# Activation transposes of the feed-forwards: from TensorE to VectorE and a round trip through device memory

## The chip, the cores and the metric
The kernel runs on one core of a Trainium2 chip: TensorE (PE) with its weight loads (PEld), VectorE (DVE), ScalarE (ACT), GpSimd (POOL), SyncE (SP) and 16 DMA engines. The metric is the device time of one execution in microseconds. Before the change it is 1530.09 us, the median of 3 runs (1528.64 to 1535.28).

## The reference
A first block (RWKV-7 time mixing and differential attention side by side, a feed-forward, and PLE, a gated addition) is followed by two layers of a second block, each a gated feed-forward, an attention stage and another gated feed-forward. There are 256 tokens of width 1024, all in fp32. What the change touches is the five feed-forwards and PLE:

```
# first block; h = rmsnorm(x, norm_mlp_g)
x = x + square(relu(h @ w_ff1)) @ w_ff2                              # 1024 -> 4096 -> 1024
x = x + (p @ w_ple) * sigmoid(rmsnorm(x, norm_ple_g) @ w_ple_gate)
# second block, four times; h = rms_norm(x, g)
x = x + 0.5 * ((silu(h @ w_gate) * (h @ w_up)) @ w_down)             # 1024 -> 2816 -> 1024
```

## The kernel before
The tokens are two tiles of 128 (t = 0, 1, the token halves). A matmul wants its contraction on the partitions, so each left factor is needed transposed: `hT`, the normed input, and `aT`, the activations of a feed-forward. Every fp32 product is made of three matmuls (`mm3`): both factors are split into a high part `hi`, rounded to the type of the fast matmul, and the rest `lo`, and hi\*hi, hi\*lo and lo\*hi are added up in PSUM.

Weights come from device memory in units of 128x1024 (512 KB). SP's queue issues their transfers into three `raw` buffers; ACT makes `hi` (L365) and DVE `lo` (L366). There are 5 + 6 = 11 pairs of hi/lo buffers; a pair comes free when PE has read its unit for the last time. An up or gate block of 512 columns is four units of two rows of blocks; a down block of 512 rows is four units.

`mlp` goes through the hidden width in chunks of 512 (one of a gated feed-forward's six is 256 wide; the first feed-forward has eight). For each chunk it makes the up product of both token halves (gate and up products in a gated one), ACT evacuates the first product with its nonlinearity (L463) and DVE multiplies (L465); the result is `a`, 128 tokens by 512. `flip_side` makes `aT` of it: four PE transposes of 128x128 into a PSUM bank (L283), then ACT's `aTh` and DVE's `aTl` out of PSUM (L365, L366). The down product of a chunk (`down`) runs one chunk late, after the up products of the next chunk, into four PSUM banks that stay held. In chunk 0 the products are ordered by token half (t outer), in the others by weight (j outer).

PE's order is written out by the program: `Weave` keeps a modelled time, and side streams such as `flip_side` are put between the matmuls of the main stream once their due time has come (3.0 us after `a` was issued). The order on the other engines is made by a scheduler, and each engine takes its instructions in order. `Normed` makes `hT`: half of x is multiplied by the gain (L909, in `FinalNorm` L1751), flipped by PE, and its reciprocal norm `r` is applied when a product is evacuated. `Ple.run` makes the gate product of token half 0 with all of `w_ple_gate` (eight units), the value products of both halves, and the gate product of half 1; `merge` adds to x.

POOL has no transfer in this kernel; its few operations are in the mixing and attention stages.

Of the kernel before, what the change touches and what calls it, by code (L numbers as in the profile page):

```python
# [7 lines left out]
F32 = mybir.dt.float32  # L8
# [4 lines left out]
AF = mybir.ActivationFunctionType  # L13
ALU = mybir.AluOpType
# [4 lines left out]
D = 1024  # L19
# [89 lines left out]
class Mark:  # L109


    def __init__(self):
        self.done, self.at, self.res = False, 0.0, None
# [105 lines left out]
class Ker:  # L219


    def __init__(self, ctx, tc, d):
        self.tc, self.nc, self.d = tc, tc.nc, d
        nc = self.nc
        ctx.enter_context(tc.manual_schedule(engines={mybir.EngineType.PE}))
        self.W = Weave()
        self.const = ctx.enter_context(tc.tile_pool(name="const", bufs=1))
        self.xp = ctx.enter_context(tc.tile_pool(name="xp", bufs=1))
        self.act = ctx.enter_context(tc.tile_pool(name="act", bufs=2))
        self.ps = ctx.enter_context(tc.tile_pool(name="ps", bufs=1, space=PSUM))  # L230
        self.banks = Slots(self.W, self.ps, "b", [128, 512], 8)
        self.quota, self.held = 2, 0
        self.x = [self.xp.tile([128, D], F32, name=f"x{t}") for t in range(2)]
        self.pre = None
# [195 lines left out]
    def flip_side(self, src, hi, lo, lat, wait=()):  # L430
# [8 lines left out]
        s.res = (hi, lo)  # L439
        return s  # L440

    def mlp(self, pool, hT, names, i, chunks, kind, res, after):

        nc, W = self.nc, self.W
        self.quota = 6
        acc = {}
        held = []
        nw = len(names) - 1  # L450
        for ci, w in enumerate(chunks):
            kt = w // 128
            ws = [self.wblock((n, i, ci)) for n in names[:-1]]
            order = [(t, j) for t in range(2) for j in range(nw)] if ci == 0 else [(t, j) for j in range(nw) for t in range(2)]
            a, aT = {}, {}
            for t, j in order:
                b = self.bank()
                p = b[1][:, :w]
                for k in range(8):
                    self.mm3(p, hT[t].at(k), ws[j][k], k == 0, k == 7)  # L460
                if j == 0:
                    a[t] = pool.tile([128, 512], F32, tag="a", name="a", bufs=4)[:, :w]
                    nc.scalar.activation(out=a[t], in_=p, func=AF.Silu if kind == "swiglu" else AF.Relu, scale=hT[t].r)  # L463
                if j == nw - 1:
                    nc.vector.scalar_tensor_tensor(out=a[t], in0=p, scalar=hT[t].r, in1=a[t], op0=ALU.mult, op1=ALU.mult)  # L465
                    th = pool.tile([128, 4, 128], F32R, tag="aTh", name="aTh", bufs=5)
                    tl = pool.tile([128, 4, 128], F32R, tag="aTl", name="aTl", bufs=5)
                    aT[t] = self.flip_side(a[t], th[:, :kt], tl[:, :kt], 3.0)
                self.drop(b, 2.0)
            held.append((kt, aT, self.wblock((names[-1], i, ci))))  # L470
            if 1 <= ci < len(chunks) - 1:
                for t in range(2):
                    self.down(acc, t, held[:1], res)
                held = held[1:]
        for t in range(2):
            self.down(acc, t, held, res, after)
# [420 lines left out]
class Normed:  # L897
# [9 lines left out]
    def half(self, s, lat=3.0):  # L907
        c = slice(s * 512, s * 512 + 512)
        self.K.nc.vector.tensor_tensor(out=self.h[:, c], in0=self.K.x[self.t][:, c], in1=self.g[:, c], op=ALU.mult)  # L909
        self.flip(s, lat)  # L910
        self.K.square(self.K.x[self.t], s, self.ss)
        if s:
            self.m, self.r = self.K.rstd(self.ss, "x")
# [29 lines left out]
def ffn_plan(names, i, chunks):  # L943

    out, off = [], 0
    for ci, w in enumerate(chunks):
        for n in names[:-1]:
            out.append(((n, i, ci), (0, D), [(off, off + w)]))
        out.append(((names[-1], i, ci), (off, off + w), [(0, D)]))
        off += w  # L950
    return out
# [89 lines left out]

def first_plan():
    out = ffn_plan(("w_ff1", "w_ff2"), 0, FF1_CHUNKS)
    out.append((("w_ple_gate", 0, 0), (0, D), [(0, D)]))
    out.append((("w_ple", 0, 0), (0, 256), [(0, D)]))
    return out


# [4 lines left out]
class Mix:  # L1053
# [193 lines left out]
    def inverse(self, H, wait):  # L1247
# [25 lines left out]
        gl = lambda q, i: G[quad[q], 4 * H + i % 4, c_of(q, i), 32 * (q % 2):32 * (q % 2) + 32]  # L1273
        at = lambda T: (lambda q, i: T[quad[q], i])
        product(reg[0], at(U), at(L))
        nc.vector.tensor_tensor(out=X, in0=reg[0], in1=X, op=ALU.add)
        yield 0.8
        product(reg[1], at(U), at(X))
        nc.vector.tensor_tensor(out=X, in0=reg[1], in1=bc(self.i32), op=ALU.add)
        nc.vector.transpose(out=Y, in_=X)  # L1280
        yield 0.9
        for lv in range(3):
            product(reg[0], gl, at(X))
            nc.scalar.activation(out=Q, in_=reg[0], func=AF.Copy)
            yield 0.8
            product(reg[1], at(Y), at(Q))
            nc.vector.copy_predicated(out=X, mask=bc(self.lvl[:, lv]), data=reg[1])
            nc.vector.transpose(out=Y, in_=X)
            yield 1.3
# [400 lines left out]
class Ple:  # L1690
# [8 lines left out]
            lo = pool.tile([128, 2, 128], F32R, name="pTl", tag="pTl", bufs=2)  # L1699
            self.flips.append(K.flip_side(pt, hi, lo, 4.0))  # L1700

    def product(self, lhs, w, evacuate):
        K = self.K
        for s in range(2):
            c = slice(s * 512, s * 512 + 512)
            b = K.bank()
            n = len(w)
            for k in range(n):
                K.mm3(b[1], lhs(k), (w[k][0][:, c], w[k][1][:, c]), k == 0, k == n - 1)
            evacuate(s, c, b[1])  # L1710
            K.drop(b)

    def run(self, pool, hT, after):
        K, nc = self.K, self.K.nc
        K.quota = 4
        wg = K.wblock(("w_ple_gate", 0, 0))
        wp = K.wblock(("w_ple", 0, 0))
        gt = [pool.tile([128, D], F32, name="pg", tag="pg", bufs=2) for _ in range(2)]
        pw = pool.tile([128, D], F32, name="pw", tag="pw", bufs=1)

        def gate(t):
            self.product(hT[t].at, wg, lambda s, c, p: nc.scalar.activation(out=gt[t][:, c], in_=p, func=AF.Sigmoid, scale=hT[t].r))

        def value(t, evacuate):
            f = K.W.need(self.flips[t])
            self.product(lambda k: (f[0][:, k], f[1][:, k]), wp, evacuate)

        def merge(t, s, c, v):
            nc.vector.tensor_tensor(out=gt[t][:, c], in0=gt[t][:, c], in1=v, op=ALU.mult)
            nc.vector.tensor_tensor(out=K.x[t][:, c], in0=K.x[t][:, c], in1=gt[t][:, c], op=ALU.add)  # L1730
            after(t, s)

        gate(0)
        value(0, lambda s, c, p: merge(0, s, c, p))
        value(1, lambda s, c, p: nc.scalar.activation(out=pw[:, c], in_=p, func=AF.Copy))
        self.product(hT[1].at, wg, lambda s, c, p: (
            nc.scalar.activation(out=gt[1][:, c], in_=p, func=AF.Sigmoid, scale=hT[1].r), merge(1, s, c, pw[:, c])))


class FinalNorm(Normed):  # L1740
# [63 lines left out]
def full_plan():  # L1804
    return mix_plan() + first_plan() + second_plan()
# [48 lines left out]
```

## Time and profile before

| | |
|---|---|
| median of 3 runs | 1530.09 us |
| profiled execution | 1529.78 us, of which the span from the first to the last instruction is 1528.0 |
| granted TensorE clock, mean | 0.994 |
| busy: PE, PEld, DVE, ACT, POOL | 1489.4, 1237.2, 927.9, 760.8, 46.7 us |
| transfers | 253.53 MB on SP's queue, 51.1% of the 16 DMA engines' time |

The stages follow each other: mixing to about 300 us, the first feed-forward to 470, PLE to 501, then layer 0 (feed-forward to 685, attention to 817, feed-forward to 1015) and layer 1 (to 1199, to 1332, to the end). Matmuls are pipelined: the profile gives one of 512 columns some 0.39 us, and they start 0.23 us apart. An engine's idle time is given with what ended it (the releaser).

### The profile page before, as it was taken

The page shows a single profiled execution, that of the slowest core. Times are in us where ns is not written, and L with a number is a line of the kernel's source. Part 1 is how long each engine was busy: PE and PEld are TensorE (multiplying, and loading weights), DVE is VectorE, ACT ScalarE, POOL GpSimd, SP SyncE. Part 2 cuts the span into 40 slices and gives each one's busy share as a digit, 9 for nine tenths or more (in the row PEclk, how much of TensorE's full clock was granted, in tenths as well). Part 3 has the DMA queues.
Part 4 walks back from the last instruction along what each step waited for, and adds up shares of the span by engine and source line. Part 5 has one row for each costly group of instructions (what it writes and reads, how often), then busy time and mean ns, then how long its engine had stood idle before and what let it go on. Part 6 is the DMA issues. An engine that isn't in the chain of part 4 may idle for free.

```text
span 1528.0 us, 22440 instructions
## 1 busy us (share of the span) xinstructions
PE 1489.4 (97%) x8804; PEld 1237.2 (81%) x8804; DVE 927.9 (61%) x1528; ACT 760.8 (50%) x1142; POOL 46.7 (3%) x70
## 2 busy tenths in 40 slices
PE   7999989999999999999999999999999999999999
PEld 6887767788888788887888888887888888888887
DVE  5886777755558755557546554566545787565552
ACT  6644445644536544447565444445444566464441
POOL 1120100000000000001100000000000010000000
PEclk9999999999999999999999999999999999999999
DMA  7233238655544765536434665547555444275551
GB/s 253 90 118 107 98 119 278 202 194 177 182 151 157 223 200 190 185 132 193 138 111 147 198 194 192 179 156 220 190 189 182 141 154 136 78 227 180 179 182 53
DMA packets 76298, 254.97 MB, mean 167 GB/s; under 512 B 11040, under 2 KB 13344, under 8 KB 76192
## 3 DMA queue, kind: packets, MB, share of 16 engines
q1 hardware_dynamic: 76192, 253.53, 51.1%
q8 instruction: 69, 1.13, 0.3%
q14 instruction: 37, 0.30, 0.1%
HBM read 252.45 MB, written 1.05 MB: 166 GB/s over the span
## 4 chain that ended last, share of the span: by engine, by line
PE 81%; DVE 7%; DMA 5%; ACT 4%; issue 2%; POOL 0%; SPq 0%; ACTq 0%; DVEq 0%; POOLq 0%
PE b L279 77%; DMA raw<-in_w_dram 4%; PE b L283 4%; DVE lo L366 2%; ACT hi L365 2%; DMA grow<-in_norm_mix_g_dram 0%; DMA stage<-in_consts_dram 0%; DMA lam<-in_lam_k_dram 0%; POOL rb L563 0%; POOL rb L562 0%; DVE hTl L366 0%; DVE c L1132 0%; DVE U L1260 0%; DVE u L1129 0%; ACT e L376 0%
## 5 line engine op out<-in xcount | busy, mean ns | idle before, releaser
L366 DVE TENSOR_TENSOR lo<-raw,hi 128x1024 fp32r<-128x1024 f32 (+1 forms) x465 | 561.9, 1214 | 356.1 <-ACT hi L365 350.1
L365 ACT ACTIVATE hi<-raw 128x1024 fp32r<-128x1024 f32 (+1 forms) x465 | 485.6, 1050 | 417.4 <-PE b L279 207.6
L279 PE MATMUL b<-hi,hTh 128*128 128x512 f32 (+2 forms) x1312 | 499.9, 381 | 0.7 <-ACT hi L365 0.7
L279 PE MATMUL b<-hi,hTl 128*128 128x512 f32 (+2 forms) x1312 | 489.9, 373 | 0.5 <-DVE hTl L366 0.5
L279 PE MATMUL b<-lo,hTh 128*128 128x512 f32 (+2 forms) x1312 | 489.7, 373 | 0.8 <-DVE lo L366 0.8
L279 PEld LDWEIGHTS b<-hi,hTl 128*128 128x128 f32 x1312 | 247.4, 189 | 47.8 <-DVE hTl L366 0.9
L279 PEld LDWEIGHTS b<-hi,hTh 128*128 128x128 f32 x1312 | 247.6, 189 | 46.1 <-issue 2.5
L279 PEld LDWEIGHTS b<-lo,hTh 128*128 128x128 f32 x1312 | 247.8, 189 | 44.2 <-DVE lo L366 1.5
L279 PE MATMUL b<-hi,aTh 128*128 128x512 f32 x480 | 191.6, 399 | 0.0
L279 PE MATMUL b<-hi,aTl 128*128 128x512 f32 x480 | 188.1, 392 | 0.0
L279 PE MATMUL b<-lo,aTh 128*128 128x512 f32 x480 | 187.4, 390 | 0.0
L279 PEld LDWEIGHTS b<-hi,aTl 128*128 128x128 f32 x480 | 90.1, 188 | 20.1
L279 PEld LDWEIGHTS b<-lo,aTh 128*128 128x128 f32 x480 | 90.3, 188 | 18.0
L279 PEld LDWEIGHTS b<-hi,aTh 128*128 128x128 f32 x480 | 90.2, 188 | 17.6
L463 ACT ACTIVATE a<-b,rsi_x 128x512 f32<-128x512 f32 (+1 forms) x52 | 34.4, 662 | 55.3 <-PE b L279 55.2
L365 ACT ACTIVATE aTh<-b 128x512 fp32r<-128x512 f32 (+1 forms) x64 | 36.3, 567 | 43.2 <-PE b L283 41.8
L465 DVE SCALAR_TENSOR_TENSOR a<-b,rsi_x,a 128x512 f32<-128x512 f32 (+1 forms) x52 | 37.2, 716 | 32.1 <-PE b L279 17.3
L366 DVE TENSOR_TENSOR aTl<-b,aTh 128x512 fp32r<-128x512 f32 (+1 forms) x64 | 41.8, 653 | 20.0 <-ACT aTh L365 19.7
L279 PE MATMUL b<-hi,hT1h 128*128 128x512 f32 (+1 forms) x128 | 53.4, 418 | 0.0
L279 PE MATMUL b<-lo,hT1h 128*128 128x512 f32 (+1 forms) x128 | 47.8, 373 | 0.6 <-DVE lo L366 0.6
L279 PE MATMUL b<-hi,hT1l 128*128 128x512 f32 (+1 forms) x128 | 47.4, 371 | 0.0
L365 ACT ACTIVATE hTh<-b 128x512 fp32r<-128x512 f32 (+1 forms) x48 | 25.2, 541 | 38.1 <-PE b L283 33.5
(582 smaller groups left out, 1293.6 us busy)
## 6 DMA issues: line engine op xcount, KB each, us to landing
raw<-in_w_dram SPq DMA_DIRECT2D x446, 512.0 KB, 4.2
raw<-in_w_dram SPq DMA_DIRECT2D x16, 384.0 KB, 3.4
grow<-in_norm_ffn_dram SPq DMA_DIRECT2D x4, 512.0 KB, 5.3
x<-in_x_dram SPq DMA_DIRECT2D x4, 256.0 KB, 6.2
x<-in_x_dram SPq DMA_DIRECT2D x2, 512.0 KB, 4.4
grow<-in_norm_mix_dram SPq DMA_DIRECT2D x2, 512.0 KB, 4.8
out_dram<-x SPq DMA_DIRECT2D x4, 256.0 KB, 2.0
raw<-in_w_dram SPq DMA_DIRECT2D x2, 396.0 KB, 3.6
```

The lines of the kernel that those rows point to most:

```text
L279: self.nc.tensor.matmul(out=out, lhsT=lhsT, rhs=rhs, start=start, stop=stop, skip_group_check=skip)
L283: self.nc.tensor.transpose(out=out, in_=src, identity=self.ident)
L365: self.nc.scalar.activation(out=hi, in_=src, func=AF.Copy)
L366: self.nc.vector.tensor_tensor(out=lo, in0=src, in1=hi.bitcast(F32), op=ALU.subtract)
L463: nc.scalar.activation(out=a[t], in_=p, func=AF.Silu if kind == "swiglu" else AF.Relu, scale=hT[t].r)
L465: nc.vector.scalar_tensor_tensor(out=a[t], in0=p, scalar=hT[t].r, in1=a[t], op0=ALU.mult, op1=ALU.mult)
```

## The change
It has three parts. `flip_moved` takes the place of `flip_side` in every chunk of a feed-forward but the last: DVE transposes the 32x32 squares within each quarter of the partitions (L449), POOL's queue stores the tile to a buffer in device memory (L451, 512 pieces of 512 bytes) and reads it back in four transfers, one for each quarter of the partitions (L453, 128 pieces of 512 bytes each; half as long in the 256 wide chunk), and ACT and DVE make `aTh` (L455) and `aTl` (L456) from SBUF. PE's modelled time takes the result as ready 9.0 us later. Then, chunk 0 is ordered by weight like the others. Last, PLE's gate weight is cut into two blocks of 512 columns, its products are ordered by half block, and all four value products go through ACT to SBUF.

```
...
+        self.dram = ctx.enter_context(tc.tile_pool(name="dram", bufs=3, space=bass.MemoryType.DRAM))
...
+    def flip_moved(self, pool, src, hi, lo):
+
+        nc = self.nc
+        n = src.shape[1] // 128
+        sq = pool.tile([128, 4, 4, 32], F32, name="fsq", tag="fsq", bufs=2)[:, :, :n]
+        to = pool.tile([128, 4, 4, 32], F32, name="fto", tag="fto", bufs=2)[:, :, :n]
+        nc.vector.transpose(out=sq.rearrange("p j k s -> p k j s"), in_=src.rearrange("p (k j s) -> p k j s", j=4, s=32))
+        mid = self.dram.tile([4, 32, 4, 128 * n // 4], F32, name="fmid", tag=f"fmid{n}")
+        nc.gpsimd.dma_start(out=mid.rearrange("i r j e -> (i r) j e"), in_=sq.rearrange("p j k s -> p j (k s)"))
+        for j in range(4):
+            nc.gpsimd.dma_start(out=to[32 * j:32 * j + 32].rearrange("r i k s -> r i (k s)"), in_=mid[:, :, j].rearrange("i r e -> r i e"))
+        v = lambda x: x.rearrange("p k (i s) -> p i k s", s=32)
+        nc.scalar.activation(out=v(hi), in_=to, func=AF.Copy)
+        nc.vector.tensor_tensor(out=v(lo), in0=to, in1=v(hi).bitcast(F32), op=ALU.subtract)
+        m = Mark()
+        m.res = (hi, lo)
+        self.W.finish(m, 9.0)
+        return m
+
 
 
     def mlp(self, pool, hT, names, i, chunks, kind, res, after):
@@ -451,7 +471,7 @@
         for ci, w in enumerate(chunks):
             kt = w // 128
             ws = [self.wblock((n, i, ci)) for n in names[:-1]]
-            order = [(t, j) for t in range(2) for j in range(nw)] if ci == 0 else [(t, j) for j in range(nw) for t in range(2)]
+            order = [(t, j) for j in range(nw) for t in range(2)]
             a, aT = {}, {}
             for t, j in order:
                 b = self.bank()
@@ -465,7 +485,10 @@
                     nc.vector.scalar_tensor_tensor(out=a[t], in0=p, scalar=hT[t].r, in1=a[t], op0=ALU.mult, op1=ALU.mult)
                     th = pool.tile([128, 4, 128], F32R, tag="aTh", name="aTh", bufs=5)
                     tl = pool.tile([128, 4, 128], F32R, tag="aTl", name="aTl", bufs=5)
-                    aT[t] = self.flip_side(a[t], th[:, :kt], tl[:, :kt], 3.0)
+                    if ci == len(chunks) - 1:
+                        aT[t] = self.flip_side(a[t], th[:, :kt], tl[:, :kt], 3.0)
+                    else:
+                        aT[t] = self.flip_moved(pool, a[t], th[:, :kt], tl[:, :kt])
                 self.drop(b, 2.0)
             held.append((kt, aT, self.wblock((names[-1], i, ci))))
             if 1 <= ci < len(chunks) - 1:
...
 def first_plan():
     out = ffn_plan(("w_ff1", "w_ff2"), 0, FF1_CHUNKS)
-    out.append((("w_ple_gate", 0, 0), (0, D), [(0, D)]))
+    out.append((("w_ple_gate", 0, 0), (0, D), [(0, 512)]))
     out.append((("w_ple", 0, 0), (0, 256), [(0, D)]))
+    out.append((("w_ple_gate", 0, 1), (0, D), [(512, D)]))
     return out
 
 
...
-    def product(self, lhs, w, evacuate):
...
+    def product(self, lhs, w):
+        K = self.K
+        b = K.bank()
+        for k in range(len(w)):
+            K.mm3(b[1], lhs(k), w[k], k == 0, k == len(w) - 1)
+        return b
...
+        def value(t, s, wp):
             f = K.W.need(self.flips[t])
...
+            nc.scalar.activation(out=pw[t][:, c], in_=b[1], func=AF.Copy)
...
-        gate(0)
-        value(0, lambda s, c, p: merge(0, s, c, p))
-        value(1, lambda s, c, p: nc.scalar.activation(out=pw[:, c], in_=p, func=AF.Copy))
-        self.product(hT[1].at, wg, lambda s, c, p: (
-            nc.scalar.activation(out=gt[1][:, c], in_=p, func=AF.Sigmoid, scale=hT[1].r), merge(1, s, c, pw[:, c])))
+        w = K.wblock(("w_ple_gate", 0, 0))
+        wp = K.wblock(("w_ple", 0, 0))
+        gate(0, 0, w)
+        for s in range(2):
+            value(0, s, wp)
+        merge(0, 0)
+        gate(1, 0, w)
+        w = K.wblock(("w_ple_gate", 0, 1))
+        gate(0, 1, w)
+        merge(0, 1)
+        for s in range(2):
+            value(1, s, wp)
+        merge(1, 0)
+        gate(1, 1, w)
+        merge(1, 1)
...
```

Lines 1 to 231 keep their numbers; below them the changed kernel's are one higher, and from `mlp` on about twenty (L463 becomes L483, L465 becomes L485, L365 and L366 become L366 and L367).

On ACT, in a middle chunk of the first feed-forward (`a` is the evacuation of a product, `hi` the split of a weight unit, `aTh` the high part of the transposed activations, out of the PSUM bank `b` or the tile `fto` that was read back). Before:

```order
L463 ACTIVATE a<-b,rsi_x 128x512
L365 ACTIVATE hi<-raw 128x1024 x2
L365 ACTIVATE aTh<-b 128x512
L365 ACTIVATE hi<-raw 128x1024
L463 ACTIVATE a<-b,rsi_x 128x512
L365 ACTIVATE hi<-raw 128x1024
L365 ACTIVATE aTh<-b 128x512
L365 ACTIVATE hi<-raw 128x1024 x4
```

And now, in the same place:

```order
L483 ACTIVATE a<-b,rsi_x 128x512
L366 ACTIVATE hi<-raw 128x1024 x3
L483 ACTIVATE a<-b,rsi_x 128x512
L366 ACTIVATE hi<-raw 128x1024
L455 ACTIVATE aTh<-fto 128x4x4x32
L366 ACTIVATE hi<-raw 128x1024 x3
L455 ACTIVATE aTh<-fto 128x4x4x32
L366 ACTIVATE hi<-raw 128x1024
```

Both `aTh` now stand behind the second evacuation, the first with one split between and the second three splits later.

On ACT, in a full chunk of a gated feed-forward, before:

```order
L463 ACTIVATE a<-b,rsi_g 128x512
L365 ACTIVATE hi<-raw 128x1024 x3
L463 ACTIVATE a<-b,rsi_g 128x512
L365 ACTIVATE hi<-raw 128x1024 x3
L365 ACTIVATE aTh<-b 128x512
L365 ACTIVATE hi<-raw 128x1024 x2
L365 ACTIVATE aTh<-b 128x512
```

And now:

```order
L483 ACTIVATE a<-b,rsi_g 128x512
L366 ACTIVATE hi<-raw 128x1024 x3
L483 ACTIVATE a<-b,rsi_g 128x512
L366 ACTIVATE hi<-raw 128x1024 x5
L455 ACTIVATE aTh<-fto 128x4x4x32
L366 ACTIVATE hi<-raw 128x1024 x2
L455 ACTIVATE aTh<-fto 128x4x4x32
```

Two more splits stand ahead of the first `aTh`; the rest of the chunk is as before.

On POOL, at the end of layer 0's first feed-forward and the attention stage behind it (`rb` is part of the attention's rotary step). Before, this is all that POOL does there:

```order
L1391 TENSOR_TENSOR z<-z,row_g_1195 128x256
L562 TENSOR_TENSOR rb<-qn,gs 128x8x32
L563 TENSOR_TENSOR rb<-qn,gs 128x8x32
L562 TENSOR_TENSOR rb<-qn,gs 128x8x32
L563 TENSOR_TENSOR rb<-qn,gs 128x8x32
```

And now (`fmid` is the buffer in device memory, `fsq` the tile that DVE transposed):

```order
L451 DMA fmid<-fsq 128x512
L453 DMA fto<-fmid 32x4x128 x4
L451 DMA fmid<-fsq 128x512
L453 DMA fto<-fmid 32x4x128 x4
L585 TENSOR_TENSOR rb<-qn,gs 128x8x32
L586 TENSOR_TENSOR rb<-qn,gs 128x8x32
```

Each flip puts five transfers on POOL's queue, one store and four reads, of which the first read waits until the store has landed; nothing else of POOL stands among them in a feed-forward.

## Rows read from the trace of the kernel before

**Rows 1.** The page, part 1: busy us (share of the span) xinstructions

```profile
PE 1489.4 (97%) x8804; PEld 1237.2 (81%) x8804; DVE 927.9 (61%) x1528; ACT 760.8 (50%) x1142; POOL 46.7 (3%) x70
```

**Rows 2.** By stage: stretch, us, busy PE, PEld, DVE, ACT, POOL, clock, DMA, GB/s

```profile
302.00:470.00 168.00, 168.00 (x769) 137.93 (x770) 94.98 (x105) 79.39 (x94) 0.00 (x0) 1.00 0.54 175
...
530.00:690.00 160.00, 160.00 (x767) 132.84 (x766) 85.18 (x94) 70.58 (x83) 0.00 (x0) 1.00 0.55 179
```

**Rows 3.** The chain that ended last: start us, us, what

```profile
308.58 16.60 PE b L279 x72
325.61 5.50 PE b L279 x24
331.55 16.58 PE b L279 x72
...
578.53 5.52 PE b L279 x24
584.49 19.76 PE b L279 x132
604.46 2.78 PE b L279 x12
```

**Rows 4.** Groups by line and shape: xcount, busy us, mean ns, idle before

```profile
L465 DVE SCALAR_TENSOR_TENSOR a<-b,rsi_x,a 128x512 f32<-128x512 f32 x46 | 34.4, 747 | 32.1 <-PE b L279 17.3 <-ACT a L463 13.6 <-ACT hi L365 1.3
L365 ACT ACTIVATE aTh<-b 128x512 fp32r<-128x512 f32 x56 | 33.2, 593 | 37.1 <-PE b L283 35.6
L463 ACT ACTIVATE a<-b,rsi_x 128x512 f32<-128x512 f32 x46 | 31.6, 686 | 53.0 <-PE b L279 52.9
L365 ACT ACTIVATE aTh<-b 128x256 fp32r<-128x256 f32 x8 | 3.1, 382 | 6.2 <-PE b L283 6.2
L1288 DVE STREAM_TRANSPOSE Y<-X 128x256 f32<-128x256 f32 x6 | 2.6, 439 | 0.0
```

**Rows 5.** Transfers: landings, SP's issue, packets; last row: 504 to 507.2 us

```profile
L341 SPq DMA_DIRECT2D raw<-in_w_dram x465: 327/328/1104, 3.5 to 1490.0; - x155
DMA to landing us min/median/max: 2.7/4.1/7.8
...
out_dram<-x SPq DMA_DIRECT2D x4, 256.0 KB, 2.0
c_nones<-in_consts_dram SPq DMA_DIRECT2D x1, 64.0 KB, 2.4
q1 hardware_dynamic: 76192, 253.53, 51.1%
...
q1 hardware_dynamic: 519, 0.20, 25.0%
```

**Rows 6.** The weight splits, then waits from 308.58 to 446.31 us: total, times, longest

```profile
L366 DVE TENSOR_TENSOR lo<-raw,hi 128x1024 fp32r<-128x1024 f32 (+1 forms) x465 | 561.9, 1214 | 356.1 <-ACT hi L365 350.1
L365 ACT ACTIVATE hi<-raw 128x1024 fp32r<-128x1024 f32 (+1 forms) x465 | 485.6, 1050 | 417.4 <-PE b L279 207.6
...
ACT hi L365 <- DMA raw<-in_w_dram: 24.5, 14, 4.3
ACT hi L365 <- PE b L279: 24.2, 27, 2.8
```

**Rows 7.** Timeline behind PLE, 510 to 516 us, then that stretch's clock

```profile
510.52 1.28 ACT L463 ACT_TABLE_LOAD   x1 [5.14 <-DVE x L1766]
511.82 0.69 ACT L463 ACTIVATE a<-b,rsi_g 128x512 f32<-128x512 f32 x1
513.43 0.66 PE L283 MATMUL b<-ident,a 128*128 128x128 f32 x4 [2.33 <-DVE a L465]
...
514.60:518.00 3.40, 3.40 (x10) 2.62 (x9) 3.11 (x4) 2.63 (x4) 0.00 (x0) 0.51 0.53 166
```

**Rows 8.** Timeline of the attention stage, POOL beside DVE

```profile
744.12 1.18 POOL L562 TENSOR_TENSOR rb<-qn,gs 128x256 f32<-128x256 f32 x1 [30.69 <-DVE qn L553]
744.62 1.76 DVE L366 TENSOR_TENSOR lo<-raw,hi 128x1024 fp32r<-128x1024 f32 x1
```

More of the change, by code (lines that the diff above doesn't have):

```diff
@@ L1700, in __init__ @@
             self.flips.append(K.flip_side(pt, hi, lo, 4.0))
-    def product(self, lhs, w, evacuate):
+    def product(self, lhs, w):
         K = self.K
[L1704 to L1711, printed above, removed]
+        b = K.bank()
+        for k in range(len(w)):
+            K.mm3(b[1], lhs(k), w[k], k == 0, k == len(w) - 1)
+        return b
     def run(self, pool, hT, after):
@@ L1715, in run, with gate, merge @@
         K.quota = 4
-        wg = K.wblock(("w_ple_gate", 0, 0))
-        wp = K.wblock(("w_ple", 0, 0))
         gt = [pool.tile([128, D], F32, name="pg", tag="pg", bufs=2) for _ in range(2)]
[L1719 to L1724, printed above, removed]
-            f = K.W.need(self.flips[t])
-            self.product(lambda k: (f[0][:, k], f[1][:, k]), wp, evacuate)
-        def merge(t, s, c, v):
-            nc.vector.tensor_tensor(out=gt[t][:, c], in0=gt[t][:, c], in1=v, op=ALU.mult)
+        pw = [pool.tile([128, D], F32, name="pw", tag="pw", bufs=2) for _ in range(2)]
+        half = lambda s: slice(s * 512, s * 512 + 512)
+        def gate(t, s, wg):
+            b = self.product(hT[t].at, wg)
+            nc.scalar.activation(out=gt[t][:, half(s)], in_=b[1], func=AF.Sigmoid, scale=hT[t].r)
+            K.drop(b)
+        def value(t, s, wp):
+            f = K.W.need(self.flips[t])
+            c = half(s)
+            b = self.product(lambda k: (f[0][:, k], f[1][:, k]), [(h[:, c], l[:, c]) for h, l in wp])
+            nc.scalar.activation(out=pw[t][:, c], in_=b[1], func=AF.Copy)
+            K.drop(b)
+        def merge(t, s):
+            c = half(s)
+            nc.vector.tensor_tensor(out=gt[t][:, c], in0=gt[t][:, c], in1=pw[t][:, c], op=ALU.mult)
             nc.vector.tensor_tensor(out=K.x[t][:, c], in0=K.x[t][:, c], in1=gt[t][:, c], op=ALU.add)
             after(t, s)
-        gate(0)
-        value(0, lambda s, c, p: merge(0, s, c, p))
-        value(1, lambda s, c, p: nc.scalar.activation(out=pw[:, c], in_=p, func=AF.Copy))
-        self.product(hT[1].at, wg, lambda s, c, p: (
-            nc.scalar.activation(out=gt[1][:, c], in_=p, func=AF.Sigmoid, scale=hT[1].r), merge(1, s, c, pw[:, c])))
+        w = K.wblock(("w_ple_gate", 0, 0))
[13 more added lines that the diff above has]
+        merge(1, 1)
 class FinalNorm(Normed):
```

## The prediction
> **What bounds the kernel now.** I read the page's busy shares first: TensorE (PE) is busy 97% of the span, VectorE (DVE) 61%, ScalarE (ACT) 50%, GpSimd (POOL) 3% [rows 1]. That is a mean over unlike stages, so the table by stage came next. In the stretch that holds the first feed-forward, and in one that holds a gated one, PE is busy for the whole of the stretch at a granted clock of 1.00, and DVE and ACT for about half [rows 2]. Then the chain that ended last, in order of time: in the feed-forwards it is nothing but PE matmuls, broken by short gaps, and each gap is a flip, the four TensorE transposes of one activation tile [rows 3]. So in these stages a microsecond taken from PE is a microsecond off the end, as long as what feeds PE keeps up.
>
> **What goes from PE.** In the first feed-forward one period of the chain runs from 308.58 to 331.55, 22.97 us; it holds 16.60 + 5.50 = 22.10 us of matmuls and two flips, so a flip costs 0.435 us. In a gated one, 578.53 + 5.52 = 584.05 to 584.49 gives 0.44; a flip of the 256 wide chunk (584.49 + 19.76 = 604.25 to 604.46) costs 0.21 [rows 3]. The number of flips: ACT evacuates 56 tiles of 512 and 8 of 256 [rows 4]. The last chunk of each of five feed-forwards keeps its two TensorE flips, all of them 512 wide, so 46 and 8 go: 46 x 0.435 + 8 x 0.21 = 21.7 us. Apart from these, the matmuls of the feed-forwards stand in the order of before.
>
> **What comes in their place.** A DVE transpose of 128x256 takes 0.44 us [rows 4]; a 128x512 one lies between that and twice it, 0.88; I take 0.70, nearer the upper end, since the shorter tile carries the same start-up. 54 of them are under 38 us on an engine that is idle half of these stages, beside PE. The hi and lo passes stay, now from SBUF. Off PE, what matters is how late a tile comes back. No row of before shows a transfer issued by POOL. SP's issue of a weight transfer takes 0.33 us, 1.10 at most; I take the upper end, because the store has 512 pieces where a weight load has 128, and keep 0.33 for the range. Small transfers land in 2.0 us (256 KB out) to 2.4 us (64 KB in), weight loads in 2.7 to 7.8, median 4.1 [rows 5]; I take 2.5 for the store and 2.8 for a read. From the start of the DVE pass that finishes the tile: 0.75 [rows 4] + 0.70 + issue 1.1 + 2.5 + four issues 4.4 + 2.8 = 12.3 us; with ACT's 0.69 before it [rows 4], 13. With SP's fast issue it is 9; with 1.10 and the slowest landing, 23.
>
> What hides it is PE's own work between a tile and its use. In the first feed-forward that is the other token half (5.5), the previous chunk's down product (11.0) and the next up product (11.0): 27.6 us; for chunk 0, which has no down product before it, 16.6; in a gated one 5.5 + 11 + 22 = 38.6 (24 matmuls are 5.5 us [rows 3]). So 13 us is hidden everywhere, 23 us everywhere but in chunk 0.
>
> **The wait that is added.** ACT takes its instructions in order, so an aTh that waits for a transfer holds the weight splits behind it, and DVE's lo behind those. By the order in the first feed-forward, ACT comes to the first aTh 7.3 us after the first evacuation (5.5 to the second, then 0.69 and one split of 1.05 [rows 4, 6]) and waits until 13: 5.7 us. Three splits later (3.2 us) it comes to the second, at 16.8; that tile is 5.5 us younger and its store stands on POOL behind four reads, some 2 us more: 20.5, a wait of 3.7. One split, and the next evacuation starts at 22.2, against 22.1 by PE. It just fits. In a gated feed-forward there are five splits ahead of the first aTh, and the waits come to some 5 us in 33.
>
> What is queued behind is the weight supply. A unit of 512 KB feeds 12 matmuls, 16.60 / 72 x 12 = 2.77 us of PE [rows 3]. It goes through one of three raw buffers: landing 4.1, hi 1.05, lo 1.21 [rows 5, 6], so 6.4 / 3 = 2.1 us a unit. ACT waits there about as long for PE to free a hi/lo buffer (24.2 us) as for a load (24.5) [rows 6]: the eleven pairs fill up, which is up to 17 us of work ahead. Eight units are 17 us of a 22.1 us chunk; the waits on ACT take some 3 us net, since three loads land during them. The supply holds, with little left.
>
> The DMA engines carry 27 MB more, in 46 x 1024 + 8 x 1024 = 55,300 pieces of 512 B or less. By bytes that adds 27 / 253.5 x 51.1% = 5.5% to their share; by pieces at the mean cost of a present packet, 37% [rows 5]. A stretch of nothing but small pieces and one weight load has 519 packets in 25.0% of 16 x 3.2 us, 25 ns each [rows 5], so 55,300 x 25 / 16 = 86 us, 5.7%: the lower end. I leave the landing at 4.1; at 37% it would go to the slow end of its row.
>
> **The other edits.** Behind the stage between the feed-forwards (PLE), PE stands 2.33 us at 513.43 for a flip of an activation that ACT evacuated only at 511.82, after 5.14 us behind DVE and a table load; then PE ran 3.4 us at a granted clock of 0.51, the lower of its two levels [rows 7]. After the change no PE instruction waits for that tile, so 2.33 + 3.4 / 2 = 4.0 us go. Against it: with the gate and up products of chunk 0 now by weight and not by token half, the second half's transposed input is wanted 5.5 us after the first half begins, not 11; in the first feed-forward, which always ran so, PE is idle nowhere in the stretch [rows 2]. PLE's new order brings two more evacuations on ACT and a later finish of the first half, with 8 us of PE work ahead. I allow 2 us for all of it (bounds: 0, and 2 us at each of four gated starts, 8).
>
> **The sum.** 1529.8 (profiled run; span 1528.0 and 1.8 around it, 0.3 under the median shown) - 21.7 - 4.0 + 2.0 = 1506.1. Its own range is 1502 (no allowance, a little from small waits) to 1514 (8 us at the starts).
>
> **Rivals.**
> Half eaten: the aTh waits come out a few us longer and the supply runs dry late in each feed-forward. For it: 22.2 against 22.1 has no slack. Against: the pairs hold up to 17 us. If each of 23 full chunks that move loses 0.5 us, 11.5 us go: 1518; between 1514 and 1530.
>
> Slower, by POOL's queue: one in-order queue takes five transfers a flip, and the reads wait for their store's landing, so a flip holds it 5 x 1.1 + 2.5 = 8.0 us. It decides beyond 11.05 us (half a chunk of 22.1) in the first feed-forward, and beyond 16.6 in the gated ones. With 2 us an issue and a landing of 5.5 it is 15.5: 14 x 4.45 = 62 us, less 17 held in the pairs, 45: 1551. At 19.3 (2.3 us an issue and the slowest landing, 7.8) both kinds of feed-forward are bound and it is over 1600. For it: no row shows POOL's issue. Against: it needs twice the slowest issue of SP's row.
>
> POOL held by DVE: in the attention stage a DVE lo beside a POOL operation takes 1.76 us, where its mean is 1.21 [rows 6, 8]. If each of the five issues had to wait out one lo of 1.2 us, a flip would hold POOL for 14 us: 14 x 3 = 42, less 17: 1531. The Trainium skill (SBUF — State Buffer, its box on how DVE blocks DMA) has such a rule: transfers issued from GpSimd have their descriptors written by GpSimd, which is locked out while VectorE runs an operation on both ports. The same page limits it, for operations with two SBUF inputs, to GpSimd work that reads SBUF; no run here yet shows an issue beside a lo.
>
> That nothing changes because the transposes hid behind matmuls is excluded by the gaps of [rows 3]; left is an unseen wait of the same size, within 0.5%.
>
> **Chances.** The forecast (up to 1514) 0.66; half eaten 0.17, of which 0.08 still clearly faster and 0.09 within 0.5%; POOL held by DVE 0.06, half of it on either side of 0.5%; POOL's queue 0.09; no net change 0.02. Half a percent, 7.7 us, is about what a measurement can tell here. Faster 0.74, same 0.14, slower 0.12. The range of 1500 to 1531 leaves out the queue case and little else.
>
> **What would show it.** Right: no transposes of a on PE before a last chunk, chunk periods of 22.1 and 33.2 us, PE without gaps; aTh waiting on ACT for fto some 4 to 6 us; POOL under 8 us a flip; no stall near 513. Wrong: PE waiting for hi, lo or aTh in the middle of a feed-forward, raw loads landing well beyond 4.1, or a POOL queue without pauses.

## The result and the profile after

The changed kernel takes 1546.4 us (median of 20 executions, 1529.2 to 1554.0) where the kernel before takes 1530.1 (20 executions). The ratio is 1.0092 with a 95% interval of 1.0074 to 1.0109: slower by some 14 us, where 24 us faster was forecast. Ratios leave out every execution more than 1.5% above its kernel's fastest: two of these twenty (1552.4 and 1554.0 us), and below one of 2908.6 us among the late split's, left out of its median too, which nothing on record explains. The first profile was taken of the fastest of the twenty, 1529.2 us, so it shows less of the loss than most executions have. A second one, of the same kernel unaltered, is of an execution with a span of 1541.6 us. It is called the second profile below, and the waits are read from it.

TensorE did lose its flips. Part 1 of the second profile's page (engine, busy us and share of the span, number of instructions) answers to [rows 1]:

```profile
PE 1475.8 (96%) x8604; PEld 1217.4 (79%) x8604; DVE 955.7 (62%) x1582; ACT 749.4 (49%) x1144; POOL 195.9 (13%) x340
```

PE has 200 instructions and 13.6 us of work fewer. But the table by stage of the second profile (stretch, its length, busy us of PE, PEld, DVE, ACT, POOL, granted clock, DMA share, GB/s), which answers to [rows 2], shows that PE does not run through the feed-forwards any more:

```profile
302.00:470.00 168.00, 165.11 (x720) 133.66 (x719) 103.89 (x124) 79.58 (x98) 32.92 (x60) 0.99 0.67 216
530.00:690.00 160.00, 153.70 (x710) 125.55 (x709) 88.53 (x101) 67.99 (x83) 24.03 (x44) 0.99 0.61 199
```

PE stands 2.9 and 6.3 us where it stood nowhere, and the DMA share rose from 0.54 and 0.55 to 0.67 and 0.61. The groups of the first profile by line and shape (count, busy us, mean ns | idle time before, and what ended it) answer to [rows 4]:

```profile
L449 DVE STREAM_TRANSPOSE fsq<-a 128x512 f32<-128x512 f32 x46 | 32.7, 710 | 1.3
L456 DVE TENSOR_TENSOR aTl<-fto,aTh 128x512 fp32r<-128x512 f32 x46 | 31.8, 691 | 114.2 <-ACT aTh L455 114.2
L455 ACT ACTIVATE aTh<-fto 128x512 fp32r<-128x512 f32 x46 | 29.0, 631 | 144.4 <-DMA fto<-fmid 144.2
```

DVE's pass takes 0.71 us. ACT stands 144 us before the 46 large aTh. What that does is best seen in one chunk of the first feed-forward: the timeline of the second profile (start, us, engine, line, output and input, count, and in brackets the idle time before and what ended it):

```profile
321.77 0.67 ACT L483 ACTIVATE a<-b,rsi_x 128x512 f32<-128x512 f32 x1
...
324.82 0.56 POOL L451 DMA_DIRECT2D fmid<-fsq  x1 [8.18 <-DVE fsq L449]
...
327.96 2.18 POOL L453 DMA_DIRECT2D fto<-fmid  x4 [2.57 <-ACT hi L366]
...
334.88 0.63 ACT L455 ACTIVATE aTh<-fto 128x512 fp32r<-128x512 f32 x1 [4.77 <-DMA fto<-fmid]
335.41 2.94 ACT L366 ACTIVATE hi<-raw 128x1024 fp32r<-128x1024 f32 x3
335.54 0.69 DVE L456 TENSOR_TENSOR aTl<-fto,aTh 128x512 fp32r<-128x512 f32 x1 [4.05 <-ACT aTh L455]
...
336.49 3.50 DVE L367 TENSOR_TENSOR lo<-raw,hi 128x1024 fp32r<-128x1024 f32 x3 [0.26 <-ACT hi L366]
```

The tile evacuated at 321.77 is back in SBUF at 334.88. In the last 4.77 us before that ACT does nothing. Of the three weight loads in flight two land meanwhile (332.35 and 334.37) and the third at 336.62, before ACT comes to it; so three splits follow without a pause, and three lo behind them. No raw buffer comes free during the wait: SP issues a load at 331.52, behind the last lo before it, and the next only at 337.74, when the first of these three lo has ended. For 6.2 us no load starts. ACT's waits in this stretch (308 to 446 us of the second profile: total us, times, longest) answer to the last two of [rows 6]:

```profile
ACT aTh L455 <- DMA fto<-fmid: 41.3, 11, 5.8
ACT hi L366 <- DMA raw<-in_w_dram: 29.8, 22, 4.5
ACT hi L366 <- DVE lo L367: 1.3, 1, 1.3
ACT a L483 <- PE b L280: 1.2, 1, 1.2
```

Before, ACT stood 24.2 us at PE for a pair to come free [rows 6], and at its evacuations it stood for PE as well (before, 308 to 446 us):

```profile
ACT a L463 <- PE b L279: 18.1, 10, 3.1
```

The weights were ahead. Now ACT does not wait for a pair once. The weights are only just in time, and late in the gated feed-forwards they are not. PE's gaps near the end of the first gated one, with the stretch behind the last of them as a row of the table by stage:

```profile
650.94 0.50 PE L280 MATMUL b<-lo,hTh 128*128 128x512 f32 x1 [0.75 <-DVE lo L367]
654.67 0.49 PE L280 MATMUL b<-hi,hTh 128*128 128x512 f32 x1 [0.91 <-ACT hi L366]
655.93 0.50 PE L280 MATMUL b<-lo,hTh 128*128 128x512 f32 x1 [0.77 <-DVE lo L367]
663.50 0.66 PE L284 MATMUL b<-ident,a 128*128 128x128 f32 x4 [2.64 <-DVE a L485]
...
664.20:667.60 3.40, 3.40 (x10) 2.60 (x9) 2.96 (x3) 1.51 (x3) 0.00 (x0) 0.51 0.64 252
```

PE waits for hi and lo, then 2.64 us for the tile of the last chunk, whose DVE instruction stands behind late lo; and then it runs 3.4 us at half clock (granted 0.51). The same waits end the other gated ones, at 982 to 999, 1180 to 1195 and 1505 to 1513; the clock falls only in the first of these stretches (granted 0.81 in the mean, 1.00 in the other two).

### The profile page after: what moved, and what is told of

It is laid out like the page before. It is cut to its first block, busy times and chain, and to the rows that moved or that the text cites. A ratio compares the mean times of both kernels' runs of the same rounds, so it can differ in the third digit from the quotient of the medians.

```text
span 1527.4 us, 22758 instructions
## 1 busy us (share of the span) xinstructions
PE 1473.6 (96%) x8604; PEld 1217.3 (80%) x8604; DVE 956.4 (63%) x1582; ACT 748.5 (49%) x1144; POOL 195.8 (13%) x340
## 5 line engine op out<-in xcount | busy, mean ns | idle before, releaser
L367 DVE TENSOR_TENSOR lo<-raw,hi 128x1024 fp32r<-128x1024 f32 (+1 forms) x465 | 557.1, 1213 | 249.7 <-ACT hi L366 245.2
L366 ACT ACTIVATE hi<-raw 128x1024 fp32r<-128x1024 f32 (+1 forms) x465 | 478.8, 1047 | 362.8 <-DMA raw<-in_w_dram 301.9
L453 POOL DMA_DIRECT2D fto<-fmid x216 | 117.5, 551 | 216.3 <-ACT hi L366 83.3
L451 POOL DMA_DIRECT2D fmid<-fsq x54 | 31.9, 591 | 735.5 <-DVE fsq L449 293.8
L456 DVE TENSOR_TENSOR aTl<-fto,aTh 128x512 fp32r<-128x512 f32 (+1 forms) x54 | 35.2, 652 | 136.8 <-ACT aTh L455 136.8
L455 ACT ACTIVATE aTh<-fto 128x512 fp32r<-128x512 f32 (+1 forms) x54 | 32.4, 600 | 174.6 <-DMA fto<-fmid 174.4
L367 DVE TENSOR_TENSOR hTl<-b,hTh 128x512 fp32r<-128x512 f32 (+1 forms) x48 | 29.2, 619 | 23.3 <-ACT hTh L366 23.3
```

Of the source, the lines that this page charges most:

```text
L366: self.nc.scalar.activation(out=hi, in_=src, func=AF.Copy)
L367: self.nc.vector.tensor_tensor(out=lo, in0=src, in1=hi.bitcast(F32), op=ALU.subtract)
L451: nc.gpsimd.dma_start(out=mid.rearrange("i r j e -> (i r) j e"), in_=sq.rearrange("p j k s -> p j (k s)"))
L453: nc.gpsimd.dma_start(out=to[32 * j:32 * j + 32].rearrange("r i k s -> r i (k s)"), in_=mid[:, :, j].rearrange("i r e -> r i e"))
L455: nc.scalar.activation(out=v(hi), in_=to, func=AF.Copy)
L456: nc.vector.tensor_tensor(out=v(lo), in0=to, in1=v(hi).bitcast(F32), op=ALU.subtract)
```

## The experiments

Medians are in us; the ratio to the kernel before, from runs on the same chip, has its 95% interval. Edits are shown against the changed kernel, unless the text names another.

**The changed kernel again.** No edit.

> The changed kernel once more, unaltered, for a second profile: the first was taken of an execution of 1529.2 us, the fastest of twenty, and the median is 1546.4. Theory S (weight supply: ACT stands at an aTh that waits for its transfer, the weight splits queue behind it, and the hi/lo pairs run empty): about 1546 again; the profile shows PE waiting for hi or lo in the later part of every feed-forward, more than the 14 us of idle time that the first profile has over the kernel before, and more stretches at half clock behind those waits. Theory P (the new order of PLE and of chunk 0 costs the time): the extra time lies between 470 and 530 and at the starts of the gated feed-forwards, and not late in them.

1543.9 us, ratio 1.0086 (1.0058 to 1.0114). The waits lie where theory S has them, as shown above. I added up what PE's matmuls stand apart beyond their usual 0.23 us in the five feed-forwards: some 45 us here, waits and stretches at half clock together.

**The other edits alone.** PLE's order and the order of chunk 0 put into the kernel before; every flip stays on TensorE (shown against the kernel before):

```
-            order = [(t, j) for t in range(2) for j in range(nw)] if ci == 0 else [(t, j) for j in range(nw) for t in range(2)]
+            order = [(t, j) for j in range(nw) for t in range(2)]
...
```

> The kernel before with only the other edits: chunk 0 ordered by weight and PLE's new order, all flips on TensorE. Theory S and the forecast: 1530 less 4.0 for the stall behind PLE plus up to 2 of allowance, 1526 to 1530. Theory P: some 15 us or more above the kernel before, 1545.

1527.3 us, ratio 0.9989 (0.9971 to 1.0006): theory P falls. PE's waits from 501 to 530 us have one row, where [rows 7] has 2.33 us, and there is no stretch at half clock behind it:

```profile
PE b L283 <- DVE a L465: 0.2, 1, 0.2
```

**No round trip.**

```
-        to = pool.tile([128, 4, 4, 32], F32, name="fto", tag="fto", bufs=2)[:, :, :n]
-        mid = self.dram.tile([4, 32, 4, 128 * n // 4], F32, name="fmid", tag=f"fmid{n}")
-        nc.gpsimd.dma_start(out=mid...
-        for j in range(4):
-            nc.gpsimd.dma_start(out=to[...
+        to = sq
```

> Leaves out the store and the four reads of each moved flip: aTh and aTl are taken straight from the tile of transposed squares, so what is computed is not the reference. No transfer of POOL is left, no wait for one, and no traffic. Theories S and T both say 1502 to 1512. Theory P: 1535 to 1546. Beside the run with the late split it gives the price of the traffic by itself: under S the two lie within 5 us.

1505.3 us, ratio 0.9834 (0.9806 to 0.9861): within a microsecond of the forecast, for a kernel whose flips leave PE and cost no transfer. The chain of matmuls that [rows 3] showed broken at every flip runs through here (start us, us, what):

```profile
559.98 90.69 PE b L280 x439
```

PE's matmuls stand apart some 6 us in the feed-forwards, about 39 less than in the second profile, and the spans differ by 1541.6 - 1503.1 = 38.5. So the round trip costs some 40 us, nearly all of it inside the feed-forwards, as waits of PE and the half clock behind them. Most of it falls in the gated ones: from its first up matmul to its last down matmul the first feed-forward takes 185.3 us in the second profile and 179.4 here, the four gated ones together 733.9 and 699.2.

**The late split.** aTh and aTl are held until behind the next chunk's evacuation:

```
...
+        def split():
+            nc.scalar.activation(out=v(hi), in_=to, func=AF.Copy)
+            nc.vector.tensor_tensor(out=v(lo), in0=to, in1=v(hi).bitcast(F32), op=ALU.subtract)
...
+                    ev = nc.scalar.activation(out=a[t], in_=p, func=...
+                    if self.late:
+                        with self.tc.issue_after(ev.ins):
+                            self.late.pop(0)()
```

> ACT's aTh and DVE's aTl are held back, by an order on ACT, until right behind the evacuation of the same token half in the next chunk, when the transfers landed long ago. PE's instructions, the transposes and the transfers are those of the changed kernel. Theory S: ACT's waits for fto go from 174 us to under 10, PE's waits for hi and lo in the feed-forwards go, and the time is that of the forecast, 1502 to 1514. Theory T (the transfers themselves slow the weight loads): waits for fto go, but PE still waits for weights; 1535 or more. Theory P: no change, about 1546.

1516.2 us, ratio 0.9897 (0.9866 to 0.9928). Some 28 us come back with all the transfers in place; theory T in its pure form falls. But it missed the forecast's range and lies 11 us above the run without the round trip, not the 5 expected there, and waits for fto stayed at 36.5 us, all in the first feed-forward: there the second half's evacuation in chunk 0 already took up the first half's tile, so each was 5.5 us old and not 22.

**The late split, mended** (shown against the late split).

```
-                    if self.late:
+                    if ci and self.late:
```

> The late split with its fault mended: in the first feed-forward it took up a tile one evacuation too early and waited 36 us for fto; now aTh stands behind the next chunk's evacuation there as well. Theory S: no wait for fto, PE's gaps in the first feed-forward go, 1510 to 1514. If what is left between it and 1505 is the traffic (+0.2 us on the landing of a load), it comes out where the run with the traffic alone does, within 4 us.

1513.8 us, ratio 0.9885 (0.9859 to 0.9911). ACT's waits from 308 to 446 us:

```profile
ACT hi L366 <- DMA raw<-in_w_dram: 48.8, 30, 5.0
ACT hi L366 <- PE b L280: 9.6, 7, 3.7
```

No wait for fto is left in the first feed-forward (11.4 us are, in the gated ones), and PE has no gap there. The other half of the expectation failed: the time lies 4.9 us above the run with the traffic alone, not within 4. And ACT waits twice as long for loads as before (24.5), and less than half as long for PE.

**The traffic alone.** All transfers go, but nothing reads what they bring:

```
-        nc.scalar.activation(out=v(hi), in_=to, func=AF.Copy)
+        nc.scalar.activation(out=v(hi), in_=sq, func=AF.Copy)
...
```

> The changed kernel with all five transfers of each moved flip, but aTh and aTl are taken from the tile of transposed squares, so nothing waits for the transfers and what is computed is not the reference. It is the price of the traffic alone, against 1505 without the transfers. Theory S (ACT's waits for fto starve the weight splits): 1505 to 1513, PE without gaps in the feed-forwards, ACT's waits for loads a little longer as these land later. Theory T (the traffic slows the loads): 1530 to 1546.

1508.9 us, ratio 0.9853 (0.9831 to 0.9874): 3.5 us over no transfers at all.

**The wait alone**, with a quarter of the traffic:

```
-        nc.gpsimd.dma_start(out=mid.rearrange("i r j e -> (i r) j e"), in_=sq...
+        nc.gpsimd.dma_start(out=mid[0], in_=sq[0:32].rearrange("p j k s -> p j (k s)"))
...
+        ev = nc.scalar.activation(out=one, in_=to[:, 0, 0, 0:1], func=AF.Copy)
+        with self.tc.issue_after(ev.ins):
+            nc.scalar.activation(out=v(hi), in_=sq, func=AF.Copy)
...
```

> The other half: the five transfers stay, each with a quarter of its pieces (one of four groups of 32 partitions is stored and read back), and before each aTh a one-column ACT instruction waits for them; aTh and aTl are taken from the tile of transposed squares, so what is computed is not the reference. A quarter of the traffic, the waits nearly whole. Theory S: ACT waits 130 to 180 us for fto, PE waits for hi and lo late in the feed-forwards, 1530 to 1545. Theory T: 1510.

1509.8 us, ratio 0.9863 (0.9841 to 0.9885): 4.5 us over none. Here theory S, as I had it, falls: ACT waited 128.6 us for the transfers, just under what was expected, and PE hardly noticed. Neither 3.5 nor 4.5 us is clear of noise: the intervals of these two ratios overlap that of the run without the round trip. So neither the traffic nor a wait of this length does the damage by itself: the whole round trip costs about 40. The wait was not whole, though: the changed kernel's is 188.4 us in the second profile, and what a wait of that length costs without the traffic no run shows. ACT's waits from 308 to 446 us suggest why the two go badly together. First without the round trip, then with the traffic alone, then with the wait alone:

```profile
ACT hi L366 <- DMA raw<-in_w_dram: 24.0, 19, 3.6
ACT hi L366 <- PE b L280: 22.3, 20, 3.7
ACT a L479 <- PE b L280: 15.2, 10, 3.0
```

```profile
ACT hi L366 <- DMA raw<-in_w_dram: 45.2, 29, 3.9
ACT hi L366 <- PE b L280: 8.3, 8, 3.6
ACT a L483 <- PE b L280: 6.8, 5, 2.9
```

```profile
ACT hi L366 <- DMA raw<-in_w_dram: 35.5, 22, 4.7
ACT one L456 <- DMA fto<-fmid: 28.2, 10, 5.0
ACT a L486 <- PE b L280: 2.3, 3, 1.0
...
ACT hi L366 <- PE b L280: 1.5, 3, 0.8
```

ACT's waiting for PE is the cover: time by which the weights are ahead. There are 22.3 + 15.2 = 37.5 us of it. The traffic takes 37.5 - 15.1 = 22 us, the wait 37.5 - 3.8 = 34. Either fits into 37.5; both, 56, don't, and by this account 19 us are missing in these six chunks. PE lost only 6 us in the first feed-forward; that weights lay ahead at its start, and that this stock went first, would explain the rest, but is not shown. In the first gated one, where more is lost, the account reads alike (530 to 650 us: without the round trip, with the traffic alone, with the wait alone):

```profile
ACT hi L366 <- PE b L280: 25.6, 19, 4.4
ACT a L479 <- PE b L280: 7.6, 6, 3.2
...
ACT hi L366 <- PE b L280: 3.2, 3, 2.2
ACT a L483 <- PE b L280: 1.9, 1, 1.9
...
ACT hi L366 <- PE b L280: 3.9, 2, 2.9
```

Of 33.2 us the traffic leaves 5.1 and the wait 3.9. I call this theory C; the next three runs test it.

**The traffic twice**, again with hi and lo made from the squares (shown against the run with the traffic alone):

```
-        for j in range(4):
+        for _ in range(2):
+            nc.gpsimd.dma_start(out=mid...
+        for j in (0, 1, 2, 3, 0, 1, 2, 3):
```

> As the run with the traffic alone (aTh and aTl from the tile of transposed squares, nothing waits, what is computed is not the reference), with the store and the four reads of each flip issued twice: twice the traffic. Once cost 3.5 us over none. Theory C: in the first feed-forward once took 22 of some 38 us for which ACT had waited for PE; twice takes 44, more than there is, so the second dose costs far more than the first: 1515 to 1540, with PE waiting for hi and lo late in the feed-forwards. If traffic adds evenly: 1512.

1542.5 us, ratio 1.0082 (1.0056 to 1.0107), just above the expected range. The first dose cost 3.5 us, the second 33.6. The gaps of PE in the first feed-forward, and the landing of the weight loads there, with twice the traffic and then with once:

```profile
393.74 0.79 PE L280 MATMUL b<-hi,hTh 128*128 128x512 f32 x1 [3.34 <-ACT hi L366]
395.19 0.80 PE L280 MATMUL b<-lo,hTh 128*128 128x512 f32 x1 [0.66 <-DVE lo L367]
447.41 0.79 PE L280 MATMUL b<-lo,hTh 128*128 128x512 f32 x1 [5.84 <-DVE lo L367]
...
DMA to landing us min/median/max: 3.5/5.2/7.5
```

```profile
DMA to landing us min/median/max: 3.2/4.4/7.2
```

The second dose is not traffic alone, though. The doubled store holds its tile longer, DVE stands for it, with the lo behind it, and ACT stands for DVE at aTh (total us, times, longest; DVE over the whole run, ACT from 308 to 446 us):

```profile
DVE fsq L449 <- DMA fmid<-fsq: 51.7, 12, 7.0
...
ACT aTh L456 <- DVE fsq L449: 29.5, 8, 5.5
```

So this run too adds a wait to traffic, and the loss lies where the wait is: from its first up matmul to its last down matmul the first feed-forward takes 208.1 us, 28.6 more than with the traffic once. In the four gated ones, where ACT stands only 4 to 11 us at aTh in each, they take 710.6 us together, 7.6 more than with the traffic once and 11.4 more than with none. There twice the traffic with little wait costs little. That fits theory C; the steep second dose by itself says nothing about traffic alone.

**Five raw buffers in the changed kernel.**

```
+        self.rawx = (ctx.enter_context(self.tc.tile_pool(name="rawx", bufs=2)), 2)
...
-    K.more_weights(ctx, 6)
+    K.more_weights(ctx, 5)
```

> The changed kernel, ACT's early aTh and its waits left as they are, with five raw buffers for weight loads in place of three from the first feed-forward on, and ten hi/lo pairs in place of eleven. Theory C (cover: a unit's way through a raw buffer, some 6.7 us, leaves little under 3 x 2.77 = 8.3 us; traffic and waits for fto each take most of the rest, and only together more than there is): the cycle has now 5 x 2.77 = 13.8 us, so nearly all comes back, 1506 to 1514, with 150 us or more of waits for fto still on ACT. Theory W (the time ACT stands idle at fto is itself what is lost): about 1540.

1511.9 us, ratio 0.9895 (0.9868 to 0.9922): 32 us come back, with ACT's waits for the round trip even longer than in the second profile (188.4):

```profile
ACT aTh L463 <- DMA fto<-fmid: 289.4, 51, 10.4
```

So ACT's standing idle is not what is lost (theory W falls). What is lost, then, is the loads that don't fly meanwhile, and with five buffers enough of them do. All of it comes back in the gated feed-forwards, which take 696.7 us together, against 733.9. The first takes 185.6, as in the second profile, now with PE waiting for an aTh near its start (1.3 us).

**Five raw buffers in the kernel before.** The same edit, against the kernel before.

> The kernel before with the five raw buffers and ten pairs. Theory C: its supply had cover left, so nothing changes, 1527 to 1532; what more raw buffers give behind the change is then no gain of their own.

1524.3 us, ratio 0.9964 (0.9951 to 0.9977), 5 us better than its neighbours, where I expected nothing. So a small part of the 32 us is a gain of its own, and the kernel before had places where it was short too. What PE's matmuls stand apart in its feed-forwards fell by about 5 us, most of it in the first gated one.

**The late split with five raw buffers.** Both edits.

> As the run with aTh behind the next chunk's evacuation, and from the first feed-forward on five raw buffers for weight loads in place of three, paid for with one of the eleven hi/lo pairs. If loads that land later are what is left over, more loads in flight hide them: 1503 to 1508. If the supply is not the bound any more, no change from the run with three, or a little slower for the lost pair.

1506.5 us, ratio 0.984 (0.9822 to 0.9859): the fastest kernel here that computes all of it, 1.6% faster than the kernel before and 2.6% faster than the changed one. It lies 1 us above the run without transfers, but that one has three raw buffers; without transfers and with five none was made. ACT's waits in the same stretch of the first feed-forward are all for PE again:

```profile
ACT hi L374 <- PE b L280: 36.8, 41, 4.6
ACT a L496 <- PE b L280: 29.1, 12, 4.5
```

## Why the prediction was wrong

**What leaves PE: right.** 21.7 us were forecast. The kernel without the round trip and the one with the other edits alone differ by the flips only: 1527.3 - 1505.3 = 22.0.

**The other edits: right in sum.** -4.0 + 2.0 was forecast; measured is -2.2 between the medians, which the interval doesn't part from zero. The stall and the half clock behind PLE are gone.

**How late a tile comes back: right, from two errors that cancel.** 13 us was forecast from ACT's evacuation; the chunk above shows 334.88 - 321.77 = 13.1, and the 14 tiles of the first feed-forward are back after 12.7 to 15.7. That the sum came out is luck. POOL issues faster than I took, 0.56 and 0.55 us against 1.1. The transfers land later, 4.3 and 4.0 against 2.5 and 2.8, in rows of the second profile that answer to [rows 5] (KB each, median us to landing):

```profile
raw<-in_w_dram SPq DMA_DIRECT2D x446, 512.0 KB, 4.3
fmid<-fsq POOLq DMA_DIRECT2D x46, 256.0 KB, 4.3
fto<-fmid POOLq DMA_DIRECT2D x184, 64.0 KB, 4.0
```

**The rivals on POOL: both fell.** A flip holds its queue 0.56 + 4.3 + 2.2 = 7.1 us, less than the 8.0 of the forecast (the longest 9.6, short of 11.05). And no read's issue is stretched by DVE, which is busy for 62% of the time beside them (min/median/max ns of the reads' issue):

```profile
L453 POOL DMA_DIRECT2D fto<-fmid x216: 551/551/584, 292.4 to 1498.3; - x108
```

The Trainium skill (SBUF — State Buffer, the box on how DVE blocks DMA) has transfers issued from GpSimd wait while DVE runs an operation on both ports. The trace shows none of it beside these two-input operations: 551 to 584 ns over all 216, of which 151 stand beside a lo. Nor do reads land later for it: the median of the 64 KB ones is 3.8 us where DVE was busy for less than half of the first 1.5 us (21 reads) and 4.1 where it was busy for 90% or more (101). Whether other operations of DVE would do it no run here shows.

**ACT's waits: larger in sum than forecast.** Forecast were 5.7 + 3.7 = 9.4 us in a chunk of the first feed-forward, and some 5 in a gated one; measured are 41.3 us in 138 (6.2 chunks), 6.6 each, and in the first gated one, from 530 to 650, 26.4 in 120, 7.3 in a chunk of 33. Over the kernel ACT stands 188 us at aTh, where 14 x 4.7 + 32 x 2.5 makes 146 by the forecast: the first feed-forward waits less than forecast, the gated ones more.

**What failed: the step on the weight supply**, "the waits on ACT take some 3 us net, since three loads land during them. The supply holds, with little left." Three things in it were wrong.
First, a unit's way through a raw buffer. I took 6.4 us from a landing of 4.1 and left that landing as it was. In the first feed-forward of the second profile it is 4.6 (median of its row there), and with 1.05 for hi, 0.2 until lo begins, 1.22 for lo and 0.03 to the next issue it makes 7.1, so 2.37 us a unit and 18.9 of the 22.1 us of a chunk, not 17. I had bounded the traffic's price and taken its lower end, since the bytes are few; but with the traffic alone ACT's waits for PE fell by 22 us in 138. How a landing 0.2 to 0.5 us later comes to that is not shown: 50 units, each later by 0.5 / 3 us, make 8 us by estimate.
Second, what a wait costs net. With three buffers and ACT standing, the loads in flight land and no further one starts until the first of the late lo ends. The wait is not absorbed by the loads: it takes their place. The run with the wait alone prices it: 28.2 us of waits took 34 us of cover.
Third, the cushion. I counted the pairs that fill up, 17 us of work ahead, against the loss; the forecast does not work that figure out, and no run measures it. It is a stock, spent once in a feed-forward, and that fits PE's gaps, most of which lie late in the gated ones.
Each burden was weighed by itself against the slack, and each alone does fit, the wait at least up to the length that was run. They were never added up against the 24.2 + 18.1 = 42.3 us for which ACT waited for PE before. The forecast also saw the tight place in the first feed-forward (22.2 against 22.1); of the 40 us that the round trip costs, 6 were lost there and 35 in the gated ones.

The rival "half eaten" named this mechanism, and by its sign (PE waits for hi and lo late in a feed-forward) it is the one that came. Its size was guessed at 0.5 us a chunk. Measured are 38.5 / 23 = 1.7 (0.8 in the first feed-forward, 2.2 in the gated ones), against the 0.9 that two flips give, and so the sign of the whole turned. No bound was worked out for it, as was done for POOL's queue: with 9.4 us of waits a chunk taken whole, on top of 8 x 2.1, the step would have come to 26 of 22.1 us.

**What stays open.** The changed kernel's twenty executions spread over 25 us, the twenty of the kernel before over 8. That a supply at its limit turns small differences in landings into gaps would fit, but no run separates it. How much of a gap is the missing weight and how much the half clock behind it was not taken apart by a run. Nor was the whole wait run without the traffic, so that part of the damage may be the wait's greater length beside the traffic, and not only the sum of the two.

## What to carry to other kernels

Where an engine issues in order and also feeds a pipeline of few buffers, a wait put on it is paid by the pipeline: ask how many loads can fly while it stands, and place the waiting instruction where its data has long landed. Before work moves to engines and queues that look idle, read the slack of what feeds the bound engine as a time (here, ACT's waits for PE), and add up everything that the change takes from it. A burden that is nearly free by itself tells nothing about two: measure both, each alone and together, and one more buffer as the cure.

## What the runs showed of the hardware

A transfer of 256 KB in 512 pieces from POOL's queue lands in 4.3 us and a read of 64 KB in 4.0 beside weight loads, where SP's small transfers landed in 2.0 to 2.4 [rows 5]; with a quarter of the pieces they take 3.3 and 3.4 us. The reads' landing follows the weight loads beside them: of the 184 reads of 64 KB in the second profile, those with fewer than one weight load in flight beside them in the mean landed in 2.2 us (44 reads), with one to two in 3.9 (84), with two or more in 5.1 (56). POOL's issue of 0.55 us lies between SP's usual 0.33 and its slowest 1.10, and hardly varies. The page counts their packets so (packets, MB, share of 16 engines' span):

```profile
q0 software_dynamic: 10976, 26.23, 5.8%
```

That is the lower end of the forecast's bounds (5.5 to 37%, taken 5.7), but not for the reason given there: not 55,300 packets of 512 B, but 11,000 of 2.4 KB in the mean (6,144 of 4 KB, 512 of 2 KB, and 4,320 of 4 bytes). This 5.8% lengthened the median landing of a load in the first feed-forward by 0.2 to 0.5 us (4.2 without transfers; 4.4 to 4.6), and twice as much by 1.0.
